# Up stages of a two-layer decoder trunk: the next pair's two plain products are written between a pair's bank copies and the products that go on in those banks

## The chip, the cores and the metric

The kernel runs on one core of a Trainium2 chip. Time is device microseconds of one execution; smaller is better. The engines are called as in the profile: PE does matrix products, PEld loads their stationary operand, DVE and ACT do elementwise work and read the banks that PE sums into, POOL does a little more elementwise work, and SP issues the transfers.

## The reference

A trunk of two layers over 1,024 tokens of 1,024 features. Layer 0 mixes tokens with a convolution module, layer 1 with sliding-window attention. Each layer then has the MLP that this change is about, and a gated embedding:

```python
def sq_relu_mlp(x, w_up, w_down):
    return jnp.square(jax.nn.relu(x @ w_up)) @ w_down

x = layer_norm(DEEPNORM_ALPHA * x + y, mix_ln_g[i], mix_ln_b[i])
x = layer_norm(DEEPNORM_ALPHA * x + sq_relu_mlp(x, mlp_w_up[i], mlp_w_down[i]),
               mlp_ln_g[i], mlp_ln_b[i])
x = x + (p[i] @ ple_w_proj[i]) * jax.nn.sigmoid(x @ ple_w_gate[i])
```

w_up has 4,096 columns, so the hidden activations are 4,096 by 1,024. Everything is float32.

## The kernel before

**Numbers.** Each float32 operand is split into a high part (a rounding copy by ACT, tiles named wh, xh and so on) and a low part (a subtraction by DVE, tiles wl, xl). One product of blocks is then three matmuls: high by high, high by low, low by high (`mm3`, line 676).

**The up stage** (`mlp`, lines 1335 to 1419) runs once for each layer. The 32 blocks of 128 hidden rows are taken two at a time: 16 pairs, f = 0, 2, ..., 30. For a pair, w_up's two blocks and both halves of the features make a 2 by 2 block matrix; the tokens' two halves and the same feature halves make another. The four results (two blocks by two token halves) come from seven block products in place of eight, by the scheme of Strassen and Winograd. Each product is four k-steps of three matmuls of 128 by 128 with 512 columns, 12 matmuls in one bank.

The seven products of a pair, by what they need:

- two plain ones, `top_left` (line 1371): u0's left half by plain[0, 0] into bank p, which ACT copies to c11; u0's right half by plain[1, 0] into another bank, which DVE adds to c11. No sums of weights or tokens are in them. Bank p is kept.
- T[2] with u1's left half goes on in p; ACT copies p to c21.
- T[3] with u2's left half begins bank r.
- T[1] with u1's right half goes on in p; ACT copies p to c22 (tag bo), and DVE adds r to c22.
- plain[1, 1] with u2's right half goes on in p; ACT squares p's positive part into c12 (tag z).
- T[4] with u3 goes on in r; DVE adds r to c21.

T[1] to T[4] are sums of token blocks, made by `token_forms` at the start of the stage. In layer 0 their tiles are named A, X, E and B. u0 to u3 are the weight units: u0 is a block as it is loaded, u1 and u2 hold sums S1 to S4 of quarters (DVE, tag g), u3 is a quarter (`pair_units`, line 1238). Each result gets relu and square (`square`, line 1204), and `keep` (line 1218) makes four more sums for the down stage and stores seven tiles to DRAM.

**Early pairs.** `EARLY` is f = 0, 2, 4, 6, 8: their two plain products all run at the head of the stage, while the token sums are made, and their p banks wait. The other 11 pairs of a layer do their plain products at the start of their own turn.

**Weight units** come through `Stream` (line 482): `add` lists them, `get` takes the next, `done` says that one more is used up, and each `done` writes the preparation of one more unit into the program. There are five slots of wh and wl, and two of the raw loads. A slot is free again when the last instruction that reads it has run.

**What sets the order.** The program only records instructions. `schedule` (line 328) then plans them all: it keeps a clock for each engine, and at each step gives the engine that is free first the earliest-written instruction whose operands are ready by modelled durations. The order of issue on each engine is fixed by that plan before the kernel runs. So the written order is a priority, and later work is pulled ahead when earlier work waits. Buffers of one tag are given out in the written order of their requests. Any two accesses of one bank, reads too, keep their written order. During the up stage the kernel has eight banks under the tags ps and tr.

Every instruction goes through line 479, so the profile has that line everywhere, and tiles and shapes tell the groups apart. For a matmul the profile names the bank, then the moving and the stationary operand: `ps<-X,wh` is T[2] in layer 0.

Of the kernel before, what the change touches and what calls it, by code (L numbers as in the profile page):

```python
# [16 lines left out]
T = 1024  # L17
# [46 lines left out]
EARLY = 0, 2, 4, 6, 8  # L64
# [447 lines left out]
class Emit:  # L512
# [822 lines left out]
    def mlp(self, i):  # L1335
        nc, d, ws = self.nc, self.d, self.ws
        tags, xtags = (dict(zip((2, 1, 3, 4), "XAEB")), "EB") if i == 0 else (dict(zip((2, 1, 3, 4), "XEAB")), "AB")
        pairs = list(range(0, NFF, 2))
        units = {}
        for f in pairs:  # L1340
            u = self.low.get((i, f)) or self.pair_units([d["w_up"][i, f + k] for k in range(2)], f in EARLY)
            units[f] = u if len(u) == 4 else u + self.pair_units([d["w_up"][i, f + k] for k in range(2)], True)[1:]
        ws.add(*[units[f][0] for f in EARLY])
        for f in pairs:
            ws.add(*units[f][f in EARLY :])

        plain = {
            (a, h): [self.xs(k + 4 * a, h * HT, HT) for k in range(4)]
            for a, h in ((0, 0), (1, 0), (1, 1))
        }  # L1350

        def prod(u, half, B, ps=None):
            wh, wl = u
            o = half * HT
            more = ps is not None
            ps = ps if more else self.ps()
            self.mm3(ps, [
                (wh[:, o + k * P : o + (k + 1) * P], wl[:, o + k * P : o + (k + 1) * P], *B[k]) for k in range(4)
            ], not more, True, more)
            return ps  # L1360

        def copy(ps, tag="t"):
            v = self.sb(tag)
            nc.scalar.copy(v, ps)
            return v

        def plus(a, ps):
            nc.vector.tensor_tensor(out=a, in0=a, in1=ps, op=ALU.add)
            return a

        def top_left(f):
            w = ws.get(1)[0]
            p = prod(w, 0, plain[0, 0])
            c = copy(p)
            p2 = prod(w, 1, plain[1, 0])
            ws.done(1)
            return p, self.square(plus(c, p2))

        for k in range(3):
            nc.move("tr", "ps")  # L1380
        banks = {}
        for f in EARLY:
            banks[f], c = top_left(f)
            self.store(i, f, (0, 0), c)
        T = self.token_forms(tags)
        self.quiet = nc.tile("xh01", (P, 4, HT), F32), nc.tile("xl01", (P, 4, HT), F32R)
        self.seven_forms(f"gate{i}", 4)
        self.seven_forms(f"down{i}", 2)

        for f in pairs:  # L1390
            early = f in banks
            if early:
                p, c11 = banks[f], self.sb("t")
                o = f % 4 // 2 * HT
                nc.sync.dma_start(c11, self.hid[i][f // 4, (0, 0)][:, o : o + HT])
            else:
                p, c11 = top_left(f)
            w12 = ws.get(1)[0]
            prod(w12, 0, T[2], p)
            c21 = copy(p)  # L1400
            w34 = ws.get(1)[0]
            r = prod(w34, 0, T[3])
            prod(w12, 1, T[1], p)
            ws.done(1)
            c22 = copy(p, "bo")
            self.square(plus(c22, r))
            w = ws.get(1)[0]
            prod(w34, 1, plain[1, 1], p)
            c12 = self.square(p, "z")
            prod(w, 0, T[4], r)  # L1410
            ws.done(2)
            self.square(plus(c21, r))
            self.keep(i, f, {(0, 0): c11, (0, 1): c12, (1, 0): c21, (1, 1): c22}, early)
            nc.slack = UP_SLACK
            if f in UP_WORK:
                self.work(UP_WORK[f][0] + str(i), UP_WORK[f][1], "Q")
            nc.slack = 0.0
            if f == MARKED:
                self.mark = nc.ops[-1]

        self.x = []
        for t in range(NT):
            self.x.append(self.pair(xtags[t // 4]))
        self.begun = set()
        self.turn = 0
        for n, cs in enumerate(DOWN):
            self.down_seven(i, cs, n == 0, n == len(DOWN) - 1, list(range(NT)) if n == RES else [])
# [666 lines left out]
```

## Time and profile before

| | |
|---|---|
| median of the three runs shown | 2133.43 us |
| the runs | 2618.16, 2131.23, 2133.43 us |
| the profiled execution, its own time | 2129.71 us |
| its span, first to last instruction | 2128.0 us |
| mean granted PE clock | 1.000 |
| up stage of layer 0 (from the first plain product to the last of T[4]) | 394.3 to 702.9 us |
| up stage of layer 1 (end taken from PE's timeline) | to 1732 us |
| HBM traffic, mean over the span | 217 GB/s |

The span is what the instructions cover; the execution's own time is 1.7 us longer. In the tables by stage, a count in brackets stands behind each engine's busy time. "Idle before" in a group is time in which the engine had nothing to run ahead of such an instruction, and the arrow names what ended it. An instruction of about 390 ns in the matmul rows overlaps the next one: the distance between two starts is what they cost.

### The profile page before, as it was taken

The page shows a single profiled execution, that of the slowest core. Times are in us where ns is not written, and L with a number is a line of the kernel's source. Part 1 is how long each engine was busy: PE and PEld are TensorE (multiplying, and loading weights), DVE is VectorE, ACT ScalarE, POOL GpSimd, SP SyncE. Part 2 cuts the span into 40 slices and gives each one's busy share as a digit, 9 for nine tenths or more (in the row PEclk, how much of TensorE's full clock was granted, in tenths as well). Part 3 has the DMA queues.
Part 4 walks back from the last instruction along what each step waited for, and adds up shares of the span by engine and source line. Part 5 has one row for each costly group of instructions (what it writes and reads, how often), then busy time and mean ns, then how long its engine had stood idle before and what let it go on. Part 6 is the DMA issues. An engine that isn't in the chain of part 4 may idle for free.

```text
span 2128.0 us, 29691 instructions
## 1 busy us (share of the span) xinstructions
PE 2111.0 (99%) x9984; PEld 1748.6 (82%) x9984; DVE 1696.3 (80%) x2750; ACT 1239.3 (58%) x2309; POOL 280.1 (13%) x494
## 2 busy tenths in 40 slices
PE   9999999999999999999999999999999999999998
PEld 7888888878888888888787888888888888888877
DVE  8767698978776879876975888699887778888688
ACT  6655654766666533335756889457666663333484
POOL 0000024100000000001421666150000000000042
PEclk9999999999999999999999999999999999999999
DMA  7778954877778747565486022777877785565726
GB/s 255 230 217 281 284 203 155 293 249 268 264 244 258 271 162 227 193 193 183 164 306 224 22 79 83 220 239 255 284 270 261 265 304 176 178 229 171 258 88 219
DMA packets 219609, 464.00 MB, mean 218 GB/s; under 512 B 22080, under 2 KB 55488, under 8 KB 219456
## 3 DMA queue, kind: packets, MB, share of 16 engines
q1 hardware_dynamic: 219456, 462.11, 65.3%
q8 instruction: 78, 1.28, 0.3%
q14 instruction: 75, 0.61, 0.1%
HBM read 314.96 MB, written 147.06 MB: 217 GB/s over the span
## 4 chain that ended last, share of the span: by engine, by line
PE 86%; DVE 4%; ACT 4%; DMA 3%; issue 1%; POOL 1%; SPq 0%; ACTq 0%; POOLq 0%; DVEq 0%
PE ps L479 67%; PE tr L479 18%; ACT z L479 2%; DMA raw<-in_w_up_dram 1%; DVE wl L479 1%; DVE g L479 1%; POOL sm L479 1%; DVE t L479 1%; ACT wh L479 1%; ACT xh L479 1%; ACT t L479 1%; DVE B L479 0%; DMA raw<-in_w_kv_dram 0%; DMA down_low_t<-xl 0%; DVE X L479 0%
## 5 line engine op out<-in xcount | busy, mean ns | idle before, releaser
L479 PE MATMUL ps<-xh,xl 128*128 128x512 f32 x618 | 240.4, 389 | 0.0
L479 PE MATMUL ps<-xl,xh 128*128 128x512 f32 x618 | 240.4, 389 | 0.0
L479 PE MATMUL ps<-xh 128*128 128x512 f32 x618 | 240.4, 389 | 0.0
L479 POOL TENSOR_SCALAR sm<-sm 128x1 f32<-128x1 f32 x72 | 27.0, 379 | 1371.3 <-DVE E L479 610.7
L479 ACT CAST wh<-raw 128x1024 fp32r<-128x1024 f32 (+2 forms) x156 | 142.1, 915 | 105.6 <-PE ps L479 43.5
L479 PE MATMUL ps<-wh,xh 128*128 128x512 f32 (+1 forms) x460 | 182.9, 398 | 2.4 <-DVE t L479 1.5
L479 PE MATMUL ps<-xh,wh 128*128 128x512 f32 x472 | 183.9, 393 | 1.1 <-ACT bo L479 0.4
L479 PE MATMUL ps<-xl,wh 128*128 128x512 f32 x472 | 184.6, 392 | 0.0
L479 PE MATMUL ps<-xh,wl 128*128 128x512 f32 x472 | 184.1, 390 | 0.0
L479 PE MATMUL ps<-wl,xh 128*128 128x512 f32 (+1 forms) x460 | 183.3, 398 | 0.3 <-DMA wl<-gate_low_t 0.3
L479 PE MATMUL ps<-wh,xl 128*128 128x512 f32 (+1 forms) x460 | 182.7, 397 | 0.0
L479 DVE TENSOR_TENSOR wl<-raw,wh 128x1024 fp32r<-128x1024 f32 (+2 forms) x100 | 98.1, 983 | 59.8 <-ACT wh L479 59.4
L479 ACT CAST xh<-wh 128x1024 fp32r<-128x1024 f32 x76 | 79.7, 1049 | 111.8 <-PE ps L479 89.3
L479 ACT CAST wh<-g 128x512 fp32r<-128x512 f32 x136 | 80.9, 620 | 109.0 <-PE ps L479 66.7
L479 PEld LDWEIGHTS ps<-xh 128*128 128x128 f32 x618 | 116.0, 188 | 24.2
L479 PEld LDWEIGHTS ps<-xh,xl 128*128 128x128 f32 x618 | 116.1, 188 | 24.0
L479 PEld LDWEIGHTS ps<-xl,xh 128*128 128x128 f32 x618 | 116.0, 188 | 24.0
L479 DVE TENSOR_TENSOR wl<-g,wh 128x512 fp32r<-128x512 f32 x136 | 89.4, 685 | 35.3 <-ACT wh L479 35.2
L479 ACT ACTIVATE t<-t 128x512 f32<-128x512 f32 x144 | 91.0, 632 | 31.1 <-DVE t L479 29.2
L479 DVE TENSOR_TENSOR xl<-wh,xh 128x1024 fp32r<-128x1024 f32 x76 | 92.7, 1219 | 20.4 <-ACT xh L479 20.4
L479 PEld LDWEIGHTS ps<-xh,wh 128*128 128x128 f32 x472 | 88.8, 188 | 21.1 <-ACT bo L479 0.8
L479 PEld LDWEIGHTS ps<-xh,wl 128*128 128x128 f32 x472 | 88.8, 188 | 18.5
(425 smaller groups left out, 5623.5 us busy)
## 6 DMA issues: line engine op xcount, KB each, us to landing
wh<-hid SPq DMA_DIRECT2D x78, 512.0 KB, 4.2
raw<-in_w_up_dram SPq DMA_DIRECT2D x68, 512.0 KB, 4.2
wl<-in_w_down_dram SPq DMA_DIRECT2D x58, 512.0 KB, 4.8
hid<-zz SPq DMA_DIRECT2D x96, 256.0 KB, 4.7
z<-in_w_dw_dram SPq DMA_DIRECT2D x64, 288.0 KB, 4.3
hid<-t SPq DMA_DIRECT2D x64, 256.0 KB, 4.5
raw<-hid SPq DMA_DIRECT2D x30, 512.0 KB, 3.9
hid<-z SPq DMA_DIRECT2D x36, 256.0 KB, 4.7
```

What stands on the lines that cost most here:

```text
L479: getattr(getattr(nc, o.eng), o.name)(*a, **k)
```

## The change

The written order of the seven products changes, and with it the order in which the weight units are listed. The next pair's two plain products are written between T[3] and T[4] of a pair. c22 is now begun as a copy of r (T[3] alone) rather than of p, and DVE adds p to it after T[1]. T[4] comes before T[1]. So r goes T[3], copy by ACT, T[4], add by DVE; p goes T[2], copy by ACT, T[1], add by DVE, plain[1, 1], square by ACT. The sums are the same. For f = 0 to 6 nothing is put between, since the next pair's plain products are early ones; for f = 8 to 28 they are put between; for f = 30 there is no next pair.

```diff
@@ -1342,7 +1342,10 @@
             units[f] = u if len(u) == 4 else u + self.pair_units([d["w_up"][i, f + k] for k in range(2)], True)[1:]
         ws.add(*[units[f][0] for f in EARLY])
         for f in pairs:
-            ws.add(*units[f][f in EARLY :])
+            ws.add(*units[f][1:3])
+            if f + 2 in pairs and f + 2 not in EARLY:
+                ws.add(units[f + 2][0])
+            ws.add(units[f][3])
 
@@ -1388,28 +1391,32 @@
         for f in pairs:
-            early = f in banks
+            early = f in EARLY
+            p = banks[f]
             if early:
-                p, c11 = banks[f], self.sb("t")
+                c11 = self.sb("t")
                 o = f % 4 // 2 * HT
                 nc.sync.dma_start(c11, self.hid[i][f // 4, (0, 0)][:, o : o + HT])
             else:
-                p, c11 = top_left(f)
+                c11 = ready
             w12 = ws.get(1)[0]
             prod(w12, 0, T[2], p)
             c21 = copy(p)
             w34 = ws.get(1)[0]
             r = prod(w34, 0, T[3])
+            c22 = copy(r, "bo")
+            if f + 2 in pairs and f + 2 not in EARLY:
+                banks[f + 2], ready = top_left(f + 2)
+            w = ws.get(1)[0]
+            prod(w, 0, T[4], r)
+            ws.done(1)
+            self.square(plus(c21, r))
             prod(w12, 1, T[1], p)
             ws.done(1)
-            c22 = copy(p, "bo")
-            self.square(plus(c22, r))
-            w = ws.get(1)[0]
+            self.square(plus(c22, p))
             prod(w34, 1, plain[1, 1], p)
+            ws.done(1)
             c12 = self.square(p, "z")
-            prod(w, 0, T[4], r)
-            ws.done(2)
-            self.square(plus(c21, r))
             self.keep(i, f, {(0, 0): c11, (0, 1): c12, (1, 0): c21, (1, 1): c22}, early)
             nc.slack = UP_SLACK
```

## The prediction

> **What bounds the kernel now.** I read the page's first lines, then the table of stages over both up stages, then who waits for whom on PE, then the timeline of one pair, and last the groups and transfers that feed it.
>
> ```profile
> span 2128.0 us, 29691 instructions
> ...
> PE 2111.0 (99%) x9984; PEld 1748.6 (82%) x9984; DVE 1696.3 (80%) x2750; ACT 1239.3 (58%) x2309; POOL 280.1 (13%) x494
> ```
>
> PE stands idle for 2128.0 - 2111.0 = 17.0 us in all. Closing waits alone, anywhere, can't bring more than that, 0.8%. The page warns that a busy PE isn't PE at its peak, so the next view counts instructions too. Its columns are the stretch and its length, then busy time and count for PE, PEld, DVE, ACT and POOL, the granted clock, DMA share and GB/s.
>
> ```profile
> 421.50:483.40 61.90, 60.79 (x266) 49.15 (x264) 47.66 (x78) 37.69 (x65) 0.00 (x0) 1.00 0.71 238
> 483.40:643.50 160.10, 160.10 (x705) 132.18 (x706) 124.84 (x195) 100.52 (x172) 0.00 (x0) 1.00 0.78 262
> 643.50:702.88 59.38, 59.26 (x262) 48.69 (x261) 40.21 (x58) 35.99 (x59) 0.00 (x0) 1.00 0.83 274
> 1426.00:1500.00 74.00, 73.84 (x335) 60.88 (x334) 67.44 (x112) 54.48 (x92) 4.92 (x6) 1.00 0.85 278
> 1500.00:1600.00 100.00, 99.89 (x440) 82.02 (x439) 80.03 (x125) 64.48 (x110) 0.00 (x0) 1.00 0.79 267
> 1600.00:1737.00 137.00, 137.00 (x606) 113.38 (x605) 100.89 (x152) 86.70 (x146) 0.00 (x0) 1.00 0.82 279
> ```
>
> The first three rows are the up stage of layer 0 behind its early top-left products, the last three that of layer 1. In the second row 705 matmuls take 160.10 us without a hole: one each 227 ns, at granted clock 1.00. A product is 12 of them, 2.72 us; a pair has seven products, 19.1 us; the 16 pairs of a stage 305 us, two stages 610 us, 29% of the span. Idle PE in these rows is 1.11 + 0.12 + 0.16 + 0.11 = 1.50 us. That is all that better cover of waits in the up stages can return. The waits behind it, for both stages:
>
> ```profile
> PE ps L479 <- ACT t L479: 0.7, 2, 0.5
> PE ps L479 <- ACT bo L479: 0.4, 1, 0.4
> ```
>
> ```profile
> PE tr L479 <- ACT z L479: 0.2, 1, 0.2
> ```
>
> Why is the wait on the bank's copy into bo, which the change goes around, seen once in 32 pairs? The timeline of PE over one pair answers it.
>
> ```profile
> 562.38 0.39 PE L479 MATMUL ps<-A,wl 128*128 128x512 f32 x1
> 562.61 0.39 PE L479 MATMUL ps<-xh,wh 128*128 128x512 f32 x1
> ...
> 564.20 0.39 PE L479 MATMUL ps<-xl,wh 128*128 128x512 f32 x1
> 564.42 0.39 PE L479 MATMUL ps<-xh,wh 128*128 128x512 f32 x1
> ...
> 566.91 0.39 PE L479 MATMUL ps<-xh,wl 128*128 128x512 f32 x1
> 567.14 0.61 PE L479 MATMUL tr<-B,wh 128*128 128x512 f32 x2
> ...
> 569.86 0.39 PE L479 MATMUL ps<-xh,wl 128*128 128x512 f32 x1
> ```
>
> ```profile
> 562.58 1.14 ACT L479 CAST wh<-g 128x512 fp32r<-128x512 f32 x2 [4.63 <-PE ps L479]
> 563.63 0.58 ACT L479 COPY bo<-ps 128x512 f32<-128x512 f32 x1
> ```
>
> The product with T[1] (in A) ends at 562.38 + 0.39 = 562.77. ACT reads its bank from 563.63 to 564.21, and the product that goes on in that bank starts at 564.42: a turnaround of 1.65 us. In it PE runs eight matmuls of the next pair's first plain product. They stop in the middle of a triple at 564.20; its missing third comes at 569.86, after the twelve that go on in the bank and the twelve with T[4] (in B). The planner, which gives PE the earliest-written instruction that is ready, already does by itself what the change writes out.
>
> **The change part by part.** Counts first: each pair keeps its 84 matmuls, two plain copies, the same bank adds, the same squares, seven stores and its loads. Nothing is added or removed, so PE's 305 us a stage stay. What moves is priced one by one.
>
> *The copy into bo* now reads r, right behind T[3], and the next pair's two plain products (24 x 227 ns = 5.45 us) are written ahead of T[4] on r. The turnaround to hide is 1.65 us, so T[4] doesn't wait. What is gained is at least nothing (the wait is hidden by the same instructions today) and at most the 1.50 us. I take 0.4, the only row that names bo: the ACT t rows are for the copies at the top of a product, which stay.
>
> *For the early pairs* 0 to 6 no products come between, so T[4] directly follows the copy of its own bank. T[1] on p is ready meanwhile, 2.72 us against 1.65: cost nothing. If that cover were gone, 1.65 x 4 pairs x 2 layers = 13 us.
>
> *The new wait.* T[1] is now followed by plain[1,1] in the same bank, with an add by DVE between. Queued behind PE's wait there is all of PE. The groups of DVE and of ACT in the steady stretch:
>
> ```profile
> L479 DVE TENSOR_TENSOR wl<-g,wh 128x512 fp32r<-128x512 f32 x26 | 17.3, 687 | 10.3 <-ACT wh L479 10.3
> ...
> L479 DVE TENSOR_TENSOR wl<-raw,wh 128x1024 fp32r<-128x1024 f32 x6 | 7.3, 1221 | 0.3 <-ACT wh L479 0.3
> ...
> L479 DVE TENSOR_TENSOR bo<-bo,ps 128x512 f32<-128x512 f32 x4 | 2.7, 680 | 0.0
> ```
>
> ```profile
> L479 ACT CAST wh<-g 128x512 fp32r<-128x512 f32 x26 | 15.4, 619 | 30.9 <-PE ps L479 26.5 <-DVE g L479 4.3
> ...
> L479 ACT CAST wh<-raw 128x1024 fp32r<-128x1024 f32 x6 | 6.3, 1055 | 2.0 <-PE tr L479 1.1 <-PE ps L479 0.9
> L479 ACT COPY bo<-ps 128x512 f32<-128x512 f32 x7 | 4.0, 577 | 0.0
> ```
>
> The add is 680 ns where the copy was 577, so the turnaround is some 1.65 + 0.10 = 1.75 us. The next pair's plain products, which fill it today, are already done then. What is left to fill it is the next pair's T[2], 2.72 us on a bank that was copied long before. I take zero; with no cover it is 1.75 x 32 = 56 us. DVE, in order, is 125/160 = 78% busy here, so a queue of two or three adds ahead of this one (2 us) belongs to the same case.
>
> *Weight slots* (five). In units of products, u1 and u2 were held for three each, u0 for two, u3 for one: 9 in 7, or 1.3 slots. Now u1 and u2 are held for six: 15 in 7, 2.1 slots. Lead from a slot's release to the next use of its successor falls from five products to four, 10.9 us, for u2 and for the next u0. What has to fit is the transfer, a cast and a subtraction.
>
> ```profile
> DMA to landing us min/median/max: 3.7/4.1/5.3
> ```
>
> At the longest 5.3 + 1.06 + 1.22 = 7.6 us, and two halves with 2 x 0.62 + 2 x 0.69 = 2.6 us for u2. Both fit in 10.9 us with at least 3.3 us over. SP's raw loads change places with result stores of the pair only, and the loads keep their order among themselves. I take zero. The other bound is a chain that the trace does show, where the early pairs end:
>
> ```profile
> 431.90 6.21 DMA raw<-in_w_up_dram
> ...
> 446.01 12.53 PE ps L479 x54
> ```
>
> From issue to PE that is 14.1 us, 3.2 over the lead; in each of the 22 pairs behind the early ones, 70 us. Nearer is the steady stretch's own row, since the 22 pairs run there. That ACT sat 26.5 us on PE in it says that slots, not transfers, set the casts' times.
>
> *Buffers and end.* r's bank is held as long as before and the next pair's two banks come sooner: about three of the eight that the stage has by its slots. The last product of a stage is now plain[1,1], so the last pair's stores go out about two adds and two ACT passes later, some 2.6 us by the rows above (an estimate). The down stage reads those chunks last: cost nothing.
>
> Sum: 2129.71 (the profiled execution; span 2128.0 and 1.71 around it) - 0.4 + 0 + 0 + 0 = 2129.3. The runs shown are 2131.23, 2133.43 and an outlier of 2618.16; the profiled one lies 3.7 under their median of 2133.43. Of the three ordinary times the middle is 2131.23, and from there the forecast is **2131 us**.
>
> **The rivals.**
>
> *Lost fill, slower.* The change uses up, ahead of time, the work that fills the turnaround behind T[1]. If T[2] of the next pair isn't ready there (its weights one product late, or DVE's add late), each pair pays up to 1.75 us: 2131 + 56 = 2187, or 2159 if half are covered. It decides from a delay of 2.72 - 1.75 = 1 us in every pair. For it: the two stages are one unbroken PE stream with 610 us, so a hole in each pair adds up. Against it: u1's slot comes free a whole pair ahead.
>
> *Late weights, slower.* 2131 + 70 = 2201 at the early pairs' price; with 1 us in each of the 22 pairs 2153.
>
> *It does nothing*, since the planner's order on PE is the same but for a few swaps: 2131, the forecast within its own noise.
>
> *PE isn't at its limit.* In the steady row PEld is busy for 132.18 of 160.10 us, 82.6%. If the loads of weights alone set the pace and a better order closed the rest, 17.4% of 610 us would go: 2025. Against it: the spacing of 227 ns holds across product borders and inside products alike, and the change alters only the order of products, not what lies inside one. The Trainium skill, Perfetto Trace Analysis, section Identifying the Most-Contended Engine, says that matmul occupancy misleads about distance to the limit and that LDWEIGHTS busy share is the better measure; no run here yet shows which holds. The Trainium skill, TensorE: Matmul & The Clock Gate, section "Wait — 56ns, not 53.3ns?", gives 215.7 ns between warm 512-column matmuls; by it 2,688 matmuls could give back 11 ns each, an estimate of 30 us and a time of 2101, but the trace's 227 ns is what these stages have, and it decides.
>
> **How the numbers follow.** Forecast with "it does nothing" 0.77 (own range 2127 to 2137: the 1.5 us bound below, spread of the ordinary runs, 4 us, either side); lost fill or late weights in part, 2137 to 2174, 0.13; one of them in full, over 2174, 0.08; PE's limit 0.02. A measurement of this kernel tells about 2% from no change, 43 us. Hence faster 0.02, same 0.90, slower 0.08. The range takes the forecast's own, widened at the bottom by 2 us for what a new plan may close of the other 15.5 us of idle, and at the top to 2150, a third of the lost fill: it leaves out 0.02 below and about 0.15 above.
>
> **What would show it.** Right: the steady stretch keeps 227 ns a matmul and PE idle of at most 2 us in the up stages; between T[1] and plain[1,1] stand matmuls of the next pair's T[2]; the plain products stand whole, 24 together, ahead of T[4]. Lost fill: a PE wait on DVE bo some 20 to 32 times with 1 to 2 us each. Late weights: PE waits on DVE wl or ACT wh, and DMA raw in the chain between 483 and 700 us. The prediction is wrong if the up stages grow or shrink by over 6 us together, or if the difference lies outside of them.

## The result, and the profile after

| | before | after |
|---|---|---|
| median, runs of each | 2131.81 us, 10 | 2138.13 us, 10 |
| ratio after to before, with its 95% interval | | 1.0025 [1.0016, 1.0034] |
| profiled execution | 2129.71 us | 2137.94 us |

The kernel became slower by a quarter of a per cent, some 5.3 us (0.0025 x 2131.81). One of the ten runs before, of 2618.16 us, and one of e2's below, of 2223.06, were slow ones and are left out of the ratios. The change is far under the 2% at which the chances were set, so "the same" came in, and 2138 lies in the range given. But the forecast said that nothing would happen, and something did: the interval excludes it.

The page of the changed kernel, same lines as before and the one on the chain that ended last:

```profile
span 2136.2 us, 29659 instructions
...
PE 2114.0 (99%) x9984; PEld 1747.4 (82%) x9984; DVE 1696.4 (79%) x2750; ACT 1242.2 (58%) x2309; POOL 280.5 (13%) x494
...
PE 81%; DMA 6%; DVE 6%; ACT 5%; issue 2%; POOL 1%; SPq 0%; DVEq 0%; ACTq 0%; POOLq 0%
```

The kernel before had this in the same place:

```profile
PE 86%; DVE 4%; ACT 4%; DMA 3%; issue 1%; POOL 1%; SPq 0%; ACTq 0%; POOLq 0%; DVEq 0%
```

PE's share of the chain falls by 5 points, and transfers and DVE gain 5: there are now stretches in which PE is not what the end hangs on. The table by stage of the changed kernel, columns and stretches as in the prediction, says which:

```profile
421.50:483.40 61.90, 60.05 (x264) 48.99 (x263) 48.88 (x80) 38.91 (x69) 0.00 (x0) 1.00 0.78 256
483.40:643.50 160.10, 159.38 (x701) 131.06 (x700) 122.53 (x193) 100.34 (x171) 0.00 (x0) 1.00 0.78 270
643.50:702.88 59.38, 59.05 (x259) 48.09 (x259) 38.91 (x58) 34.31 (x57) 0.00 (x0) 1.00 0.60 211
1426.00:1500.00 74.00, 73.70 (x335) 60.31 (x334) 65.62 (x108) 51.93 (x88) 5.33 (x7) 1.00 0.82 273
1500.00:1600.00 100.00, 98.18 (x430) 79.79 (x429) 80.22 (x126) 63.24 (x108) 0.00 (x0) 1.00 0.81 269
1600.00:1737.00 137.00, 135.81 (x594) 110.89 (x593) 96.81 (x147) 85.01 (x140) 0.00 (x0) 1.00 0.74 257
```

The granted clock is 1.00 in every row, as before. PE does fewer matmuls in the same time: 701 for 705 in the second row, 430 for 440 and 594 for 606 in the last two. Lining up the two traces by the number of the matmul, the changed kernel loses 2.3 us in the up stage of layer 0 and 5.7 in that of layer 1, gains 1.2 us ahead of the first, and differs by 1.4 us in all the rest. The two executions' spans differ by 8.2 us; the medians, by 6.3. The profiled execution of the kernel before, at 2129.71 us, was faster than any of its ten runs, so this pair of profiles shows more than the ratio does.

One measure is used below for all kernels. *PE's lost time* is the sum, over the matmuls of the two up stages, of what the distance between two starts exceeds 227 ns. It is 4.3 us before (2.8 in layer 0 and 1.5 in layer 1) and 12.2 us after (5.0 and 7.1). The longest waits of PE in the changed kernel, layer 0 and then layer 1 (engine, tile written, what it waited for: us in total, times, longest):

```profile
PE ps L479 <- ACT bo L479: 1.7, 1, 1.7
PE ps L479 <- DVE bo L479: 0.5, 2, 0.3
PE tr L479 <- DVE bo L479: 0.4, 1, 0.4
...
PE tr L479 <- DVE v L479: 1.2, 1, 1.2
PE ps L479 <- DVE z L479: 1.0, 1, 1.0
PE tr L479 <- DVE z L479: 0.4, 1, 0.4
```

The tag of c22 holds tiles named bo, z and v. With the short restarts behind them, 5.8 of the 12.2 us stand ahead of plain[1,1], behind DVE's add into c22: the wait that the change adds. Another 3.1 us stand ahead of T[4], behind ACT's copy of r into c22. The kernel before had neither. There plain[1,1] waited for ACT's copy, 1.3 us, and T[4] for DVE's add of r, 0.6 us. PE's timeline where it waits for the add, in layer 1 (T[1] in E, T[2] in X):

```profile
1624.87 0.39 PE L479 MATMUL ps<-E,wl 128*128 128x512 f32 x1
1625.09 0.62 PE L479 MATMUL ps<-X,wh 128*128 128x512 f32 x2
1625.55 0.39 PE L479 MATMUL ps<-X,wl 128*128 128x512 f32 x1
1625.77 0.61 PE L479 MATMUL ps<-X,wh 128*128 128x512 f32 x2
1627.43 0.50 PE L479 MATMUL ps<-xh,wh 128*128 128x512 f32 x1 [1.04 <-DVE z L479]
...
1630.28 0.39 PE L479 MATMUL ps<-X,wl 128*128 128x512 f32 x1
```

T[1] ends at 1624.87 + 0.39 = 1625.26, and plain[1,1] starts 2.17 us later. Five matmuls of the next pair's T[2] stand in between. The other seven could have run, but stand behind plain[1,1] on PE, from 1630.28 on. DVE over the same time:

```profile
1623.15 0.69 DVE L479 TENSOR_TENSOR zz<-t,zz 128x512 f32<-128x512 f32 x1 [1.33 <-DMA hid<-zz]
1623.76 0.69 DVE L479 TENSOR_TENSOR xl<-xh,xl 128x512 fp32r<-128x512 f32 x1
1624.36 0.68 DVE L479 TENSOR_TENSOR t<-t,tr 128x512 f32<-128x512 f32 x1
1624.96 1.22 DVE L479 TENSOR_TENSOR wl<-raw,wh 128x1024 fp32r<-128x1024 f32 x1
1626.09 0.68 DVE L479 TENSOR_TENSOR xl<-xh,xl 128x512 fp32r<-128x512 f32 x1
1626.69 0.68 DVE L479 TENSOR_TENSOR z<-z,ps 128x512 f32<-128x512 f32 x1
```

The add into c22 (tile z) starts at 1626.69, 1.43 us after its bank was complete. It isn't slow; it stands in a queue that has run without a gap since DVE stood at 1621.82 for 1.33 us, waiting for a store of zz to leave its tile. This is the rule and not the exception: of the seven places where PE waits for this add, DVE's last stop ahead of the add is at a store of zz in six. Here DVE had also stood 3.98 us for a load, until 1612.36, twenty instructions ahead of the add.

The longest wait of the changed kernel is of the other kind. It lies in an early pair of layer 0, f = 2. The rows are of DVE, of ACT and of PE (T[3] in E, T[1] in A, T[4] in B):

```profile
438.72 0.69 DVE L479 TENSOR_TENSOR g<-raw 128x512 f32<-128x512 f32 x1 [4.23 <-DMA raw<-in_w_up_dram]
...
439.45 1.82 ACT L479 CAST wh<-g 128x512 fp32r<-128x512 f32 x3 [1.93 <-DVE g L479]
441.18 0.61 ACT L479 CAST xl<-xh 128x512 fp32r<-128x512 f32 x1
441.70 0.58 ACT L479 COPY bo<-ps 128x512 f32<-128x512 f32 x1
...
439.14 0.39 PE L479 MATMUL ps<-E,wl 128*128 128x512 f32 x1
...
440.05 0.61 PE L479 MATMUL ps<-A,wh 128*128 128x512 f32 x2
442.33 0.73 PE L479 MATMUL ps<-B,wh 128*128 128x512 f32 x2 [1.66 <-ACT bo L479]
```

DVE stands 4.23 us for a load, ACT stands 1.93 us for the sum that DVE then makes, and the copy of r starts 2.17 us after T[3] ended at 439.14 + 0.39 = 439.53. Of T[1]'s twelve matmuls five stand ahead of T[4] in the fixed order.

So the question is what makes DVE late. Its waits in the steady stretch of layer 0, the kernel before first, then the changed one:

```profile
DVE wl L479 <- ACT wh L479: 27.7, 20, 2.6
...
DVE g L479 <- DMA raw<-in_w_up_dram: 1.6, 3, 0.8
```

```profile
DVE g L479 <- DMA raw<-in_w_up_dram: 19.0, 9, 4.2
...
DVE wl L479 <- ACT wh L479: 2.6, 3, 1.2
```

DVE is as busy as before (122.5 for 124.8 us) and idles as much, but for another reason: it waited for ACT's casts, and now it stands at the first sum of weights, in each of the nine pairs of the stretch, until the load has landed. The loads themselves got hardly slower (3.7/4.1/5.3 us before, minimum, median and maximum):

```profile
DMA to landing us min/median/max: 3.6/4.3/5.9
```

### The profile page after: what moved, and what is told of

Read it like the earlier page. It is cut to its first block, busy times and chain, and to the rows that moved or that the text cites. A ratio compares the mean times of both kernels' runs of the same rounds, so it can differ in the third digit from the quotient of the medians.

```text
span 2136.2 us, 29659 instructions
## 1 busy us (share of the span) xinstructions
PE 2114.0 (99%) x9984; PEld 1747.4 (82%) x9984; DVE 1696.4 (79%) x2750; ACT 1242.2 (58%) x2309; POOL 280.5 (13%) x494
## 4 chain that ended last, share of the span: by engine, by line
PE 81%; DMA 6%; DVE 6%; ACT 5%; issue 2%; POOL 1%; SPq 0%; DVEq 0%; ACTq 0%; POOLq 0%
PE ps L479 64%; PE tr L479 17%; DMA raw<-in_w_up_dram 2%; ACT z L479 2%; DMA hid<-zz 1%; DVE wl L479 1%; DVE g L479 1%; POOL sm L479 1%; DVE t L479 1%; ACT wh L479 1%; DVE zz L479 1%; DMA wh<-hid 1%; ACT xh L479 1%; DVE B L479 0%; ACT t L479 0%
## 5 line engine op out<-in xcount | busy, mean ns | idle before, releaser
L479 PE MATMUL ps<-xh 128*128 128x512 f32 x636 | 247.4, 389 | 0.0
L479 PE MATMUL ps<-xl,xh 128*128 128x512 f32 x636 | 247.4, 389 | 0.0
L479 PE MATMUL ps<-xh,xl 128*128 128x512 f32 x636 | 247.4, 389 | 0.0
L479 PE MATMUL ps<-wh,xh 128*128 128x512 f32 (+1 forms) x420 | 165.6, 395 | 2.2 <-DVE t L479 1.5
L479 PE MATMUL ps<-wl,xh 128*128 128x512 f32 (+1 forms) x420 | 166.2, 396 | 0.5 <-DMA wl<-gate_low_t 0.5
L479 PE MATMUL ps<-wh,xl 128*128 128x512 f32 (+1 forms) x420 | 165.9, 395 | 0.0
L479 DVE TENSOR_TENSOR wl<-raw,wh 128x512 fp32r<-128x512 f32 (+2 forms) x100 | 97.9, 982 | 23.0 <-ACT wh L479 21.9
L479 DVE TENSOR_TENSOR t<-t,ps 128x512 f32<-128x512 f32 (+1 forms) x145 | 82.3, 569 | 40.0 <-PE ps L479 22.4
```

The source lines that it names most:

```text
L479: getattr(getattr(nc, o.eng), o.name)(*a, **k)
```

## The experiments

Three causes were on the table: the lost cover behind T[1]; loads that come later than the plan assumes, so that DVE stands; and stores that hold DVE's tiles. `schedule` gives a load of 512 KB 1400 + 1656 ns = 3.06 us when no other transfer is in its way, worked out from its code, where the trace has 4.1 to 4.3. As the order on each engine is fixed ahead, an instruction that is planned at 3.06 us behind its load keeps all of its engine waiting for the rest. The ratios, each to the kernel before on the same chip and with its 95% interval; the waits are those of DVE for raw loads in the steady stretch, 483 to 650 us:

| run | ratio | PE's lost time, us | DVE on loads, us |
|---|---|---|---|
| before, first profile | 1 | 4.3 | 1.6 |
| after | 1.0025 [1.0016, 1.0034] | 12.2 | 19.0 |
| e1, after, the sum s4 in a tile of its own | 1.0031 [1.0020, 1.0042] | 8.9 | 12.9 |
| e2, after, all transfers planned longer | 0.9987 [0.9979, 0.9996] | 3.1 | 10.9 |
| e3, order of T[1] and T[4] alone | 1.0020 [1.0012, 1.0029] | 8.1 | 7.7 |
| e4, move of the plain products alone | 1.0023 [1.0011, 1.0034] | 6.9 | 8.3 |
| e5, after, loads planned longer | 0.9986 [0.9977, 0.9995] | 3.6 | 4.3 |
| e6, after, stores planned longer | 1.0003 [0.9994, 1.0012] | 9.0 | 18.4 |
| e7, before, all transfers planned longer | 0.9972 [0.9963, 0.9981] | 2.3 | 1.4 |
| e8, after with T[1] ahead of T[4] | 0.9996 [0.9988, 1.0005] | 5.7 | 10.7 |
| e9, before again | 1.0001 [0.9992, 1.0009] | 8.1 | 2.0 |
| e10, after again | 1.0025 [1.0014, 1.0036] | 13.3 | 20.3 |
| e11, e8 with all transfers planned longer | 0.9966 [0.9953, 0.9978] | 0.9 | 4.7 |
| e12, before, loads planned shorter | 1.0032 [1.0020, 1.0045] | 12.6 | 8.7 |

The last two columns come from one profiled execution of each kernel, and that can lie off the kernel's median: e6's took 2138.31 us and was the slowest of its eleven, e3's took 2133.63 and was the second fastest of eleven.

**e1.** The sum s4 goes to a new tile; before, it was written over s2, behind s2's store.

```diff
-        nc.vector.tensor_tensor(out=s2, in0=c[1, 0], in1=s2, op=sub)
-        self.store(i, f, "s4", s2)
+        s4 = self.sb("z")
+        nc.vector.tensor_tensor(out=s4, in0=c[1, 0], in1=s2, op=sub)
+        self.store(i, f, "s4", s4)
```

> The changed kernel, with the sum s4 written into a tile of its own instead of over s2, whose store is still being read. Store theory (the in-order DVE waits at s4 and at the next pair's s1 for a store of the zz tile to land, so the add on a product's bank comes late and PE stands): DVE's waits on stores of zz fall from 13.5 us in the two up stages to under 2, PE's lost time there from 11.8 us to about 7, and the ratio to the kernel before falls from 1.0025 to about 1.0005. Load theory (DVE waits for late weight loads, 62 us in the two stages against 17 before): DVE's waits on loads stay at about 60 us, PE's lost time at 10 us or more, the ratio at 1.002 or more.

The waits for the store of zz, 13.5 us over both stages of the changed kernel, are gone entirely, and with them most of what PE lost behind the add into c22: 1.8 us in place of 5.8. The time is no better: 1.0031 against 1.0025, in overlapping intervals. PE lost 2.9 us in place of 1.7 ahead of T[1], behind ACT's copies of p into c21. The loads are waited for as they were. In layer 1:

```profile
DVE g L479 <- DMA raw<-in_w_up_dram: 26.5, 10, 3.7
```

It was 28.5 us in the same stretch after. So the stops at stores settle at which places PE waits, but taking them away doesn't take the loss away.

**e2.** The plan counts every transfer issued in the pair loop as 1.3 us longer. Instructions and sums are those of the changed kernel; only the planned order differs.

```diff
-                finish(o, lanes[-1])
+                finish(o, lanes[-1] + o.late)
...
+        nc.late = 1300.0
         for f in pairs:
...
+        nc.late = 0.0
```

> The changed kernel; the planner counts every transfer that the pair loop issues 1.3 us longer than its model does, so that it no longer expects a load or a store before it lands. If late transfers of either kind are the cause, because DVE's order was fixed for transfers that were modelled too short: DVE's waits on transfers in the up stages fall from 75 us to under 30, PE's lost time to about 4 us as before the change, the ratio to 1.000. If the written order itself is the cause (too little work ready behind T[1]), nothing changes: 1.002 to 1.003.

2128.57 us against 2131.24: the loss is gone, and the kernel is slightly faster than before. DVE's waits on loads and zz stores over both stages fell to 41 us, less far than the under 30 that was expected (they were 75).

**e3 and e4** make one half of the change each. e3 has only the new order of T[4] and T[1], with c22 begun from r; the plain products stay at the start of their own pair:

```diff
             r = prod(w34, 0, T[3])
+            c22 = copy(r, "bo")
+            w = ws.get(1)[0]
+            prod(w, 0, T[4], r)
+            ws.done(1)
+            self.square(plus(c21, r))
             prod(w12, 1, T[1], p)
             ws.done(1)
-            c22 = copy(p, "bo")
-            self.square(plus(c22, r))
-            w = ws.get(1)[0]
+            self.square(plus(c22, p))
             prod(w34, 1, plain[1, 1], p)
+            ws.done(1)
             c12 = self.square(p, "z")
-            prod(w, 0, T[4], r)
-            ws.done(2)
-            self.square(plus(c21, r))
```

> Only the second half of the change: c22 begins from r, T[4] comes before T[1], plain[1,1] is last; the pair's two plain products stay at its own start, and the weight units keep the old order. Store theory: the sums at the end still bunch, the stores of zz are still waited for, ratio 1.001 to 1.0025. Load theory (units held longer, loads later): loads are waited for 17 to 25 us as before, ratio 1.000.

e4 moves only the next pair's plain products behind T[3]; T[1], its copy, plain[1,1] and T[4] follow as they did:

```diff
             r = prod(w34, 0, T[3])
+            if f + 2 in pairs and f + 2 not in EARLY:
+                banks[f + 2], ready = top_left(f + 2)
             prod(w12, 1, T[1], p)
             ws.done(1)
             c22 = copy(p, "bo")
             self.square(plus(c22, r))
```

> Only the first half of the change: the next pair's two plain products and its unit u0 are moved behind T[3]; c22 is copied from p, T[4] is last, as before. Store theory: stores of zz are waited for 7 us as before, ratio 1.000 to 1.0005. Load theory: DVE's waits on loads stay near 60 us and the ratio near 1.002.

Each half alone costs as much as the whole (1.0020 and 1.0023), so the two costs do not add, and neither half is the harmless one. DVE's waits on loads over both stages are 31 us in e3 and 35 in e4, between the 17 before and the 62 after; neither theory had that. Here PE's waits are mostly on ACT's copies rather than DVE's adds. Of e3 in layer 0, and of e4 in layer 1:

```profile
PE tr L479 <- ACT t L479: 1.6, 1, 1.6
PE ps L479 <- ACT bo L479: 0.8, 1, 0.8
```

```profile
PE tr L479 <- ACT t L479: 1.4, 1, 1.4
PE ps L479 <- ACT z L479: 0.5, 1, 0.5
```

The first row of each is T[1] of the stage's last pair, behind the copy of p into c21. The kernel before has such a wait too, 1.6 us at its longest in e9. The second rows are T[4] behind the copy of r, and plain[1,1] behind the copy of p. A reading: in e3 T[4] stands right behind the copy of its own bank; in e4 T[4] waits for the add that follows p's copy, and the next pair's plain products are already used, so only T[2] is left behind T[1]. In both, one product at most covers some turnaround. This is argued from the written order; no run isolates it, and what e3 and e4 lose isn't located: e4's profile has 6.9 us of lost time, e9's, of the kernel before, 8.1.

**e5 and e6** split e2: only transfers into SBUF, or only those to DRAM, are planned 1.3 us longer.

```diff
-                finish(o, lanes[-1])
+                finish(o, lanes[-1] + o.late * (isinstance(o.outv[0], View) and o.outv[0].buf.space == "SB"))
```

> The changed kernel; in the pair loop only transfers into SBUF (weight loads and the like) are planned 1.3 us later, stores as before. If the planner's short loads alone are the cause: 0.9985 to 0.9995, as with loads and stores together. If the ring of both kinds of transfer through DVE is the cause: between, 1.000 to 1.002, with DVE still waiting 8 us or more on stores of zz.

> The changed kernel; in the pair loop only transfers to DRAM (the stores of results and of weight forms) are planned 1.3 us later, loads as before. If short loads alone are the cause: 1.002 to 1.003 as the changed kernel, DVE waiting 50 us or more on loads. If stores are: 0.999 to 1.000, DVE waiting under 5 us on stores of zz.

The loads by themselves give all of it: 0.9986, as much as e2, with PE's lost time at 3.6 us, and DVE's waits on loads in the steady stretch down from 19.0:

```profile
DVE g L481 <- DMA raw<-in_w_up_dram: 4.3, 3, 2.5
```

The stores by themselves give a part, 1.0003, about 2 thousandths better than after and between the two forecasts, with DVE's waits on loads unchanged (18.4). PE's time behind the add into c22 is 1.1 us there; why the gain is as large as it is, no run shows.

**e7** asks whether the longer plan repairs something of the change, or is a gain of its own: e2's edit on the kernel before.

> The kernel before, with every transfer of the pair loop planned 1.3 us later. If the later plan only heals what the changed order broke: 0.999 to 1.001, since PE lost just 4 us in these stages. If it is a gain of its own, of the same size in both orders: 0.996, which PE's 4 us of lost time leave no room for (0.998 is the least).

0.9972, below the 0.998 that was thought the least. It is a gain of its own, 2.8 thousandths on the kernel before and 3.8 on the changed one. The table by stretch, both up stages, e7 first and before second:

```profile
421.50:707.00 285.50, 285.50 (x1261) 236.06 (x1260) 218.13 (x335) 180.34 (x306) 0.00 (x0) 1.00 0.76 259
1426.00:1740.00 314.00, 313.19 (x1387) 258.14 (x1386) 247.94 (x384) 205.11 (x348) 4.94 (x6) 1.00 0.80 267
```

```profile
421.50:707.00 285.50, 284.27 (x1249) 233.43 (x1248) 216.83 (x335) 177.73 (x302) 0.00 (x0) 1.00 0.78 261
1426.00:1740.00 314.00, 313.73 (x1391) 258.77 (x1390) 251.36 (x391) 207.27 (x349) 4.92 (x6) 1.00 0.82 276
```

In layer 0 PE has no idle time left, 1261 matmuls for 1249. The least was set by the 4.3 us of lost time in one fast profile; e9, below, shows that the same kernel can lose 8.1.

**e8** undoes one thing in the changed kernel: T[1] is written ahead of T[4] again. The plain products stay moved, and c22 stays begun from r.

```diff
-            w = ws.get(1)[0]
-            prod(w, 0, T[4], r)
-            ws.done(1)
-            self.square(plus(c21, r))
             prod(w12, 1, T[1], p)
             ws.done(1)
             self.square(plus(c22, p))
+            w = ws.get(1)[0]
+            prod(w, 0, T[4], r)
+            ws.done(1)
+            self.square(plus(c21, r))
```

> The changed kernel with T[1] written before T[4], so that twelve matmuls of T[4] stand between T[1] and plain[1,1] beside the next pair's work. Lost fill (PE has too little behind T[1], whatever made DVE late): waits of PE on the add into c22 go, 4 to 5 of the 7.7 us come back, 1.000 to 1.0008. DVE as the bound (a ring of transfers and sums as long as a pair): DVE is as late as before and PE waits elsewhere, 1.0015 to 1.003.

The whole loss goes: 0.9996 against 1.0025, with the planned durations as they were. PE's timeline of e8, in layer 0 (T[1] in A, T[4] in B, T[2] in X), shows what the order changes:

```profile
509.18 0.39 PE L479 MATMUL ps<-A,wl 128*128 128x512 f32 x1
509.41 0.61 PE L479 MATMUL ps<-B,wh 128*128 128x512 f32 x2
...
512.13 0.61 PE L479 MATMUL ps<-X,wh 128*128 128x512 f32 x2
512.58 0.39 PE L479 MATMUL ps<-X,wl 128*128 128x512 f32 x1
512.81 0.39 PE L479 MATMUL ps<-xh,wh 128*128 128x512 f32 x1
```

Behind T[1], the twelve matmuls of T[4] and three of T[2] stand ahead of plain[1,1]: 15, or 3.4 us, where the changed kernel had five, 1.1 us, at the place shown before. In most other pairs of e8 it is T[4] alone: twelve, or 2.7 us. It doesn't always do: in layer 1 PE still waits for the add into z and v, 1.1 and 1.4 us, once each, even behind a whole T[4]. DVE is still late (10.7 us on loads); it is only hidden better.

The order does a second thing. All of T[1] now stands between the copy of r and T[4], in the early pairs too. By these profiles both gaps gain alike: PE loses 3.6 us behind the add into c22 in place of 5.8, and 0.5 us ahead of T[4] in place of 3.1. So e8 shows what the place of T[4] costs, and not that it costs it behind the add alone. That the waits on the add would go was not borne out.

**e9 and e10** repeat the two kernels unchanged, for the spread of a profile.

> The kernel before once more, for a second profile on this chip and for the spread: ratio 0.9995 to 1.0005; PE's lost time in the two up stages 3 to 6 us as in the first profile (4.3).

> The changed kernel once more: ratio 1.0016 to 1.0034; PE's lost time in the up stages 9 to 14 us (12.2 in the first profile), some half of it behind the add of a bank into c22; DVE's waits on weight loads 50 to 70 us.

The ratios come back (1.0001, 1.0025). PE's lost time does not: before has 8.1 us in place of 4.3, where 3 to 6 were expected, and after 13.3 for 12.2. Differences of 4 us between two single profiles are within what one kernel shows. They are not an error of the measure: the profiled execution of e9 took 2133.61 us, 3.9 more than the first one's 2129.71, and its lost time is 3.8 more. The second pair differs by 13.3 - 8.1 = 5.2 us, the ratio's 5.3; the first, by 7.9. DVE's waits on loads repeat (2.0 and 20.3), and so does PE's time behind the add into c22, 6.8 us after 5.8, and ahead of T[4], 3.6 after 3.1.

**e11** is e8 and e2 together; **e12** is the opposite of e5 on the kernel before: loads planned 1.0 us shorter.

> The changed order with T[1] written before T[4], and every transfer of the pair loop planned 1.3 us later. Theory that late loads reach PE through DVE where the plan leaves too little between: both remedies take away the same loss, so together no more than the better one on this order, 0.997 to 0.999. If the two heal different losses: 0.9955 to 0.9965, since 0.9986 and 0.9996 against 1.0025 would add.

> The kernel before, with the transfers into SBUF of the pair loop planned 1.0 us sooner than its model has them. If a plan that expects loads too soon is what costs time, whatever the order: 1.001 to 1.003, DVE's waits on loads up from 17 us to 35 or more. If only the changed order costs: 0.999 to 1.0005.

e11 is the fastest: 2127.38 us against 2134.0. Its ratio lies just above what "the two gains add" gave, and its interval reaches into both forecasts. The intervals of e11 and e7 overlap, so it isn't shown that the moved products bring anything beyond the longer plan. e12 costs 1.0032, no less than the change, without touching the written order, and DVE waits 40 us on loads over both stages; 1.001 to 1.003 and 35 us or more were forecast. The stretches of e11, then e12:

```profile
421.50:707.00 285.50, 285.50 (x1261) 236.43 (x1260) 218.05 (x334) 181.49 (x306) 0.00 (x0) 1.00 0.75 260
1426.00:1740.00 314.00, 313.75 (x1392) 259.55 (x1391) 246.32 (x383) 205.93 (x346) 4.93 (x6) 1.00 0.80 266
```

```profile
421.50:707.00 285.50, 281.52 (x1234) 230.57 (x1233) 213.29 (x331) 175.10 (x297) 0.00 (x0) 1.00 0.76 256
1426.00:1740.00 314.00, 309.81 (x1372) 254.23 (x1371) 245.68 (x381) 200.36 (x339) 8.58 (x9) 1.00 0.80 267
```

e11 leaves PE 0.25 us of idle time in 599.5; e12 has 8.2. In e12 most of it, 6.7 us of 12.6 lost, stands behind ACT's copies into t, and 1.4 behind DVE: here, as at 442.33 above, lateness reaches PE through ACT. DVE's waits by themselves don't order the runs: e11 waits 40 us on loads over both stages too, and PE loses 0.9. A wait costs only where it ends behind PE's cover.

Read as a table, in thousandths against before:

| | order of before | order of after | e8's order |
|---|---|---|---|
| plan as it was | 0 | +2.5 | -0.4 |
| transfers planned 1.3 us longer | -2.8 | -1.3 | -3.4 |

Writing T[4] ahead of T[1] costs 2.9 in one plan and 2.1 in the other. The longer plan gives 2.8, 3.8 and 3.0. Moving the plain products costs nothing in either when c22 is begun from r and T[4] stands right behind T[1], as in e8; moved by themselves, in e4, they cost 2.3. The six entries were not all taken on one chip, so differences of half a thousandth are not read. What is shown is what repeats in this table: the price of T[4] ahead of T[1], in two plans, and the worth of longer planned transfers, in three orders. Each run's plan is another order on every engine, and the single runs e3, e4 and e6 show changes of two thousandths that no wait shown here explains.

## Why the prediction was wrong

By its own sign, up stages that "grow or shrink by over 6 us together", the first pair of profiles has it wrong, with 8.0 us; the second pair, e9 and e10, has 5.2.

**The new wait: the step that failed.** It says: "What is left to fill it is the next pair's T[2], 2.72 us on a bank that was copied long before. I take zero". The parts were right: matmuls of T[2] do stand in the turnaround, and the turnaround by the rows is 1.75 us. The comparison was wrong twice. First, not all of the 2.72 us are cover. The order is fixed by the plan, and the plan, seeing the add finished by its own durations, set plain[1,1] behind five to eight of T[2]'s twelve matmuls in 27 of the 32 pairs; the rest can't step in when the add is late. Cover is what stands ahead of the waiting instruction in the fixed order (1.1 to 1.8 us), not what would be ready. Second, the turnaround was 2.17 us at the place shown, since the add stood 1.43 us in DVE's queue. The prediction had "a queue of two or three adds ahead of this one (2 us)" in the same case and priced it at nothing. Together they put 5.8 of the changed kernel's 12.2 lost us there, and 6.8 of 13.3 in the repeat. The zero should have been about 6 us. That the whole loss is this term isn't shown: e1 leaves 1.8 us of it and is no faster, e8 leaves 3.6 and has lost nothing.

**The rival Lost fill** named this mechanism and its sign. Its sizes were for every pair, 56 us, or half, 28. The waits came in about eight pairs of 32, not in 20 to 32, and the time of 2138 is at the bottom of "in part, 2137 to 2174", which had 0.13. Its deciding point, 1 us of delay, was too late, since it too counts all of T[2] as cover: five to eight matmuls, 1.1 to 1.8 us, are about the turnaround of 1.75 or less. What it also lacked is that DVE is late enough in few pairs only.

**Weight slots.** "Both fit in 10.9 us with at least 3.3 us over. I take zero." The weights did fit: PE stands idle for ACT's wh once, for 0.2 us. The other bound, 14.1 us from issue to PE at 446.01, isn't a price of weights alone, since what ended PE's wait there is ACT's copy into bo, 0.4 us. But the step asked only whether weights reach PE in time. The loads hurt on the way there: sums of weights are planned where the plan expects the load to have landed, and DVE stands at them 19.0 us in place of 1.6, with the add for PE in its queue and, as at 442.33, ACT's casts and copies waiting for DVE. That loads were planned too short is shown by e5 and e12, in both directions. It was open to the prediction: the landing of 4.1 us was quoted there, and the planner's 3.06 us could have been worked out from its code. That much of e2's gain has nothing to do with this change is e7's finding.

**The copy into bo.** The gain of 0.4 us was not found: plain[1,1] no longer waits for the copy, which cost it 1.3 us, but T[4] does, for 3.1; the longest wait on a copy into bo is now 1.7 us, where it was 0.4. The bound of 1.50 counts PE's idle time alone. A wait that shows 1.04 us idle takes 1.31 us with its restart (1627.43), and e7 gains 0.28%, some 6 us, in the same written order.

**For the early pairs** the step fails as the first did: "T[1] on p is ready meanwhile, 2.72 us against 1.65: cost nothing." Five of T[1]'s twelve matmuls stand ahead of T[4] in each early pair of layer 0, 1.1 us, and the copy of r started 2.17 us late at the place shown. T[4] lost 2.3 us in the early pairs of both layers, 2.9 in the repeat. e8, with all of T[1] ahead of T[4], has 0.5 there.

**Buffers and end.** The down stages kept their length, as forecast. The last pair's turnarounds, with no next pair to fill them, cost about 1.5 us of PE's lost time in both layers together, behind ACT's copies: small, but not the nothing that the step has.

**What held.** Nothing outside the up stages changed by more than 1.4 us; the clock stayed 1.00; matmuls outside waits keep 227 ns. *PE isn't at its limit* fell. e11 has PE busy for 599.25 of 599.5 us and PEld for 236.43 + 259.55 = 496.0, or 82.7%, and its rate is one matmul in 226 ns (599.5 / 2653). The Trainium skill, Perfetto Trace Analysis, section Identifying the Most-Contended Engine, takes the busy share of weight loads, beside the share of peak FLOP/s, for the measure of distance to the limit, and not matmul busy time; here the 17% that it leaves were not there to be had by any order that was tried.

**In the sum**, then: "0" for the new wait stands for about +6 us, the early pairs' zero for +2 to +3, and the last pairs' for about +1.5. What goes is 1.3 us ahead of plain[1,1] and 0.6 ahead of T[4]. In the first pair of profiles this is 5.8 + 3.1 - 1.3 - 0.6 = 7.0 of the 12.2 - 4.3 = 7.9 us; in the second it is 6.8 + 3.6 - 2.1 - 1.2 = 7.1 where the difference is 5.2, so other waits shrank by 1.9. It was known that PE had 15.5 us of idle time elsewhere, and that bounded the gains; nothing bounded the losses but the cover, and the cover was counted too high.

## What to carry to other kernels

Where the order on each engine is fixed ahead, count as cover only the instructions that stand ahead of the waiting one in that order, and compare them with the turnaround plus the lateness of the engine that reads the bank. Before reordering, compare the plan's durations with the trace: here 1.3 us more on the loads gained, and 1.0 us less lost, at least as much as the whole reordering cost. An engine that carries both the operands' preparation and the reading of banks can hand a late transfer on to PE, as DVE and ACT did here.

## What the runs showed of the hardware

The same load of 512 KB, on one queue and in one stage, takes from 3.6 to 5.9 us to land, with a median of 4.3, though the DMA engines are busy for 0.78 of the time there. And two profiles of one kernel, whose times agree to 0.2% (2129.7 and 2133.6 us), differ in PE's lost time by a factor of two (4.3 and 8.1 us): the small waits differ from one execution to the next by as much as these kernels do, and only the medians told the kernels apart.
